# Fourier stage on sums and differences of mirrored tokens, its tables split once into DRAM, and one quarter of the last layer's gate and up weights left unsplit

## The chip, the cores and the metric

One core of one Trainium2 chip runs the program. The metric is the device time of one execution in microseconds (us); less is better. The engines are named as in the profile: PE (TensorE, matmuls), PEld (its weight loads), DVE (VectorE), ACT (ScalarE), POOL (GpSimd), SP (the engine whose queue starts most transfers).

## What is computed

The reference is two blocks on 1024 tokens of 1024 features with 256 context tokens. The first block (attention, RWKV and an MLP) is hardly touched here. The second has two layers; each projects the normalised tokens, mixes them in three ways (a gated chunk MLP, a Fourier mix, attention with four heads), projects back and adds 16 experts that each choose 128 tokens. What the change touches is the Fourier mix and the experts:

```python
def fourier_mix(pf):
    b, n, _ = pf.shape
    f = pf.reshape(b, n, FNET_GROUPS, FNET_GROUP_DIM).astype(jnp.float32)
    y = jnp.fft.fft2(f, axes=(1, 3), norm="ortho").real
    return y.reshape(b, n, FNET_W).astype(pf.dtype)

def chunk_mlp(pu, pv, sgu_norm, w_sgu, b_sgu):
    b, n, _ = pu.shape
    u = jax.nn.gelu(pu)
    v = rms_norm(jax.nn.gelu(pv)) * sgu_norm
    v = v.reshape(b, n // CHUNK, CHUNK, SGU_HEADS, SGU_HEAD_DIM)
    z = jnp.einsum('hpq,bcqhd->bcphd', w_sgu, v) + b_sgu.T[:, :, None]
    return u * z.reshape(b, n, SGU_W)

def expert_choice_moe(h, w_router, w_gate, w_up, w_down):
    ...
    xs = jax.vmap(lambda hb, ib: hb[ib])(h, idx)
    hid = jax.nn.silu(jnp.einsum('becd,edf->becf', xs, w_gate)) * jnp.einsum('becd,edf->becf', xs, w_up)
    y = jnp.einsum('becf,efd->becd', hid, w_down) * g[..., None].astype(h.dtype)
```

The Fourier mix takes 256 features in four groups of 64: a transform over the 1024 tokens (and one over the 256 context tokens in layer 0, since the last layer does not need the context), then one over the 64 features of a group, of which the real part stays.

## The kernel before, in words

All values are float32. Most products run in three parts: an operand is split into a rounded half (type fp32r, a cast on ACT) and the rest (a subtraction on DVE), by `split` (L75), and `mm3` (L85, its matmuls are the lines L87, L88, L89) adds high x high, high x low and low x high in PSUM.

A layer of the second block runs as `mixers` (L254: `project_in`, L606, for ten token tiles of 128; then `spatial`, L657; then the attention heads, whose preparation `prep`, L394, turns and normalises queries and keys), `project` (L764: output projection and router), and `experts` (L1002). The order of a stage's instructions on each engine is set by a scheduler that moves ready work ahead of work that waits, except in `experts`, where it is written by hand.

`spatial` holds the Fourier mix and the gate of the chunk MLP. For each of 8 token tiles it loads a 128x512 piece of the cosine table and one of the sine table (`table`, L691: into `draw`, two buffers, split to `dh`, `dl`, three each), and multiplies both with the two feature halves of the tile: 4 outputs `px`, each summed over the 8 tiles in a PSUM bank of its own, 96 matmuls of 512 columns a layer. Only 512 of the frequencies are computed; the others follow by symmetry, and frequency 512 comes from two-column matmuls with an alternating sign vector (`zps`, L706, L707). Then the four `px` are split and multiplied with small 64x64 tables on a block diagonal (`p2`), and written to DRAM as rows of `cat`. The gate (4 heads), the turning of its product `u` and the `p2` products all share one PSUM bank, `zps`. In layer 0 a small copy of the transform follows for the context. All of it stands between the last transposes of `project_in` (`nat`, L650) and the first attention scores (`SA`). Head 0's preparation is called behind `spatial` (two lines below L464) and its PSUM tiles `tps` are another pool of three banks, so the scheduler mixes its matmuls with those of the stage.

`experts` streams the weights through a ring of buffers `raw`, 512 KB for a piece of 2x128 rows and 512 columns; an expert has 12 pieces: 8 of gate and up, alternating in pairs of k, with 4 of down. `fetch` (L1013) issues loads on SP in that order as buffers come free, `cut` (L1023) splits a piece 5 ahead of its use, on ACT and DVE, each fourth on POOL instead of DVE:

```python
h, lo = (xp.tile([P, 2, 512], F32R, name=n, bufs=NS) for n in ("wh", "wl"))
nc.scalar.copy(h, raw)
(nc.gpsimd if ahead or i % 4 == 3 else nc.vector).tensor_tensor(lo, raw, asf(h), op=OP.subtract)
```

`moe_bufs` (L146) holds for each layer the buffers of the ring beside four early ones (18 and 19), of the halves (6) and the pieces that are cut ahead (5). `up` (L1070) multiplies the chosen tokens, gathered by an indirect transfer on POOL (`gather`, L1039) and turned (`turn`, L1045), with gate and up into `pg` and `pu`.

In the first block the part of the input projection that feeds RWKV (L1412) runs over seven groups of columns, whose weights are loaded and split one group ahead.

Of the kernel before, what the change touches and what calls it, by code (L numbers as in the profile page):

```python
# [17 lines left out]
P = 128  # L18
# [124 lines left out]
class Block2(Base):  # L143
    NE = 16
    moe_early = (0, 4)
    moe_bufs = ((18, 6, 5), (19, 6, 5))  # L146
    def consts2(self, pool, dram):
        self.dram = dram
        self.catd = dram.tile([1024, 1280], F32, name="catd")[:]
        for n, s in (("selr", [P, 16]), ("cosC", [P, 8, 64]), ("sinS", [P, 8, 32])):  # L150
            if not hasattr(self, n):
                setattr(self, n, self.load(pool, n, s))

# [100 lines left out]
    def mixers(self, l, last, lp, xin, cin, crows):  # L254
# [209 lines left out]
        self.spatial(l, last, TQ, f, u2, gv, ssv, sgun, bsg)  # L464
# [141 lines left out]
    def project_in(self, t, only_kv, h, fin, wp, pp, W, cqh, cql, ckh, ckl, kr, sskr, f, u2, gv, ssv, qln, kvln):  # L606
# [50 lines left out]
    def spatial(self, l, last, TQ, f, u2, gv, ssv, sgun, bsg):  # L657

        nc, ins = self.nc, self.ins
        with self.pool(f"g{l}", side="right") as cp, self.pool(f"gps{l}", space=PSUM) as pp:  # L660
# [4 lines left out]
            rv = self.rsqrt(cp, ssv[:, :TQ], TQ, 1.0 / 256, 4e-6)  # L665
            gh, gl = (cp.tile([P, TQ, 256], F32R, name=n) for n in ("gh", "gl"))
            for t in range(TQ):
                nc.vector.scalar_tensor_tensor(gv[:, t], gv[:, t], rv[:, t:t + 1], sgun, op0=OP.mult, op1=OP.mult)
                self.split(gh[:, t], gl[:, t], gv[:, t])
            ws = cp.tile([P, 512], F32, name="draw", bufs=2).rearrange("p (a b) -> p a b", a=4)  # L670
            nc.sync.dma_start(ws, ins["w_sguT"][l])
            wsh, wsl = (cp.tile([P, 4, P], F32R, name=n) for n in ("wsh", "wsl"))
            self.split(wsh, wsl, ws)
            dft, dfh = {}, {}
            for n in ("dftCd", "dftSd") + (() if last else ("dftCdc", "dftSdc")):
                dft[n] = self.load(cp, n, [P, P])
                dfh[n] = [cp.tile([P, P], F32R, name=n + m) for m in "hl"]
                self.split_v(*dfh[n], dft[n])
# [3 lines left out]
            alt = self.load(cp, "alt", [P, 2])  # L682
            altr = cp.tile([P, 2], F32R, name="altr")
            nc.vector.tensor_copy(altr, alt)

            def fpair(t):
                h, lo = (cp.tile([P, 2, 256], F32R, name=n, bufs=2) for n in ("fh", "fl"))
                self.split(h, lo, f[:, t:t + 2])
                return h, lo

            def table(src, shape):  # L691
                raw = cp.tile([P, 512], F32, name="draw", bufs=2)
                raw = raw if len(shape) == 2 else raw.rearrange("p (a b) -> p a b", a=2)
                nc.sync.dma_start(raw, src)
                th, tl = (cp.tile(shape, F32R, name=m, bufs=3) for m in ("dh", "dl"))
                self.split(th, tl, raw)
                return th, tl
            for t in range(8):
                if t % 2 == 0:
                    fh, fl = fpair(t)  # L700
                tb = [table(ins[n][t * P:t * P + P, :], [P, 512]) for n in ("dftC", "dftS")]
                for k in range(2):
                    s = slice(k * P, k * P + P)
                    for j in range(2):
                        self.mm3(pX[2 * k + j], fh[:, t % 2, s], fl[:, t % 2, s], tb[j][0], tb[j][1], t == 0, t == 7)
                    nc.tensor.matmul(pN[:, k, :], fh[:, t % 2, s], altr, start=t == 0 and k == 0, stop=False, skip_group_check=True)  # L706
# [30 lines left out]
            for k in range(2):  # L737
                for g0 in range(0, TQ, 4):
                    n = min(4, TQ - g0)
                    ps = pp.tile([P, 4, P], F32, name="zps")  # L740
                    for i in range(n):
                        nc.tensor.transpose(ps[:, i, :], u2[:, g0 + i, k * P:k * P + P], self.ident)
# [1495 lines left out]
```

## Time and profile before

| | us |
|---|---|
| three runs | 4342.38, 4343.26, 4361.83 |
| median of the runs | 4343.26 |
| the profiled execution's own time | 4345.66 |
| its span, first to last instruction | 4343.8 |
| PE busy in it | 3939.3 |
| DVE busy | 2828.5 |
| ACT busy | 1834.9 |
| POOL busy | 1072.7 |

Busy times are of one execution; the engines work beside each other, so they don't add up to the span. A share over the whole span is an average over stages with different limits, so the change is read from the windows of its own stages. In a row of the trace "us" is from an instruction's start to its end; PE's matmuls overlap, so the distance from one start to the next is what one of them costs. "<-" behind an idle time names what ended it. The granted clock of PE is a share of its full speed.

### The profile page before, as it was taken

To read this page: it belongs to the slowest core of one execution; us is meant where nothing else is said; L and a number is where in the kernel's file an instruction comes from. 1 tells how busy PE (TensorE), PEld (TensorE's weight loads), DVE (VectorE), ACT (ScalarE), POOL (GpSimd) and SP (SyncE) were. 2 spreads that over 40 slices of the span, in tenths; PEclk is the share of its full clock that TensorE was granted. 3 is DMA by queue.
4 is the path that set the end of the run, shared out by engine and by line. 5 is a ranking of instruction groups with operands and counts; after the bars stand their busy time and mean duration, and the time that the engine had idled before them with its cause. 6 is when DMAs were issued, how large, how long until landed. Compare 5 with 4: busy or idle time off the path is not lost. (4 is left out here: it accounts for less than half of the span.)

```text
span 4343.8 us, 69748 instructions
## 1 busy us (share of the span) xinstructions
PE 3939.3 (91%) x27068; PEld 3164.2 (73%) x27068; DVE 2828.5 (65%) x5419; ACT 1834.9 (42%) x3590; POOL 1072.7 (25%) x868
## 2 busy tenths in 40 slices
PE   7998989899889999999988899969997979995988
PEld 5874467777657888888967788747775868874776
DVE  5365657677676644445475566677877556666988
ACT  4234334444433311111144566325664346633665
POOL 1000012223222101101031222434544112234554
PEclk9999989999999999999999999989998989997999
DMA  6226755556462323222030202448996020146996
GB/s 244 66 89 192 234 140 129 152 125 132 86 216 108 123 82 98 93 83 68 20 126 24 73 11 66 163 175 291 304 312 201 15 71 12 69 133 227 333 345 204
DMA packets 433204, 611.91 MB, mean 141 GB/s; under 512 B 93888, under 2 KB 259920, under 8 KB 431976
## 3 DMA queue, kind: packets, MB, share of 16 engines
q1 hardware_dynamic: 403800, 527.74, 37.6%
q0 software_dynamic: 29072, 79.70, 6.7%
q8 instruction: 213, 3.49, 0.3%
q14 instruction: 119, 0.97, 0.1%
HBM read 510.29 MB, written 97.05 MB: 140 GB/s over the span
## 5 line engine op out<-in xcount | busy, mean ns | idle before, releaser
L1028 DVE TENSOR_TENSOR wl<-raw,wh 128x1024 fp32r<-128x1024 f32 x284 | 432.3, 1575 | 23.7 <-ACT wh L1027 23.4
L1027 ACT CAST wh<-raw 128x1024 fp32r<-128x1024 f32 x384 | 386.8, 1052 | 86.9 <-PE pg L89 53.0
L1028 POOL TENSOR_TENSOR wl<-raw,wh 128x1024 fp32r<-128x1024 f32 x100 | 265.6, 2661 | 289.4 <-ACT wh L1027 267.6
L87 PE MATMUL pu<-z,uh 128*128 128x256 f32 x1024 | 293.8, 287 | 4.6 <-ACT uh L77 4.6
L89 PE MATMUL pu<-z,ul 128*128 128x256 f32 x1024 | 291.2, 284 | 2.1 <-DVE ul L78 2.1
L88 PE MATMUL pu<-hl,uh 128*128 128x256 f32 x1024 | 291.2, 284 | 0.0
L2070 DVE TENSOR_TENSOR x<-x,pd 128x512 f32<-128x512 f32 x256 | 174.1, 685 | 128.2 <-PE pd L89 128.2
L2042 POOL TENSOR_TENSOR raw<-raw,g 128x1024 f32<-128x1024 f32 x32 | 82.3, 2589 | 639.6 <-DMA raw<-w_mlp_down 639.6
L87 PE MATMUL gps<-wh,hh 128*128 128x512 f32 (+2 forms) x656 | 224.0, 342 | 15.0 <-ACT hh L77 12.3
L89 PE MATMUL gps<-wh,hl 128*128 128x512 f32 (+2 forms) x656 | 220.7, 337 | 0.5 <-POOL hl L1363 0.5
L87 PEld LDWEIGHTS pu<-z,uh 128*128 128x128 f32 x1024 | 197.8, 193 | 14.8 <-issue 5.4
L87 PE MATMUL pd<-dh,ah 128*128 128x512 f32 x512 | 199.8, 390 | 2.2 <-DVE x L2070 2.0
L89 PEld LDWEIGHTS pu<-z,ul 128*128 128x128 f32 x1024 | 197.8, 193 | 2.5 <-DVE ul L78 2.4
L88 PE MATMUL pd<-dl,ah 128*128 128x512 f32 x512 | 199.4, 389 | 0.0
L89 PE MATMUL pd<-dh,al 128*128 128x512 f32 x512 | 199.2, 389 | 0.0
L88 PEld LDWEIGHTS pu<-hl,uh 128*128 128x128 f32 x1024 | 197.9, 193 | 0.1
L77 ACT CAST wh<-raw 128x512 fp32r<-128x512 f32 (+1 forms) x120 | 73.5, 614 | 200.8 <-PE gp L88 77.5
L87 PEld LDWEIGHTS gps<-wh,hh 128*128 128x128 f32 x656 | 129.8, 198 | 29.7 <-ACT hh L77 13.6
L77 ACT CAST dh<-raw 128x1024 fp32r<-128x1024 f32 x32 | 32.2, 1048 | 282.2 <-PE pd L89 276.2
L2059 DVE TENSOR_TENSOR r<-r 128x512 f32<-128x512 f32 x64 | 55.6, 868 | 142.8 <-ACT ah L2058 142.8
L89 PEld LDWEIGHTS gps<-wh,hl 128*128 128x128 f32 x656 | 129.2, 197 | 14.0 <-POOL hl L1363 0.8
L78 DVE TENSOR_TENSOR ptl<-tps,pth 128x512 fp32r<-128x512 f32 (+1 forms) x200 | 110.2, 588 | 34.9 <-ACT pth L77 33.5
(680 smaller groups left out, 12005.5 us busy)
## 6 DMA issues: line engine op xcount, KB each, us to landing
araw<-w_ada SPq DMA_DIRECT2D x144, 512.0 KB
raw<-w_gate SPq DMA_DIRECT2D x128, 512.0 KB
raw<-w_up SPq DMA_DIRECT2D x128, 512.0 KB
raw<-w_down SPq DMA_DIRECT2D x128, 512.0 KB
raw<-w_in SPq DMA_DIRECT2D x100, 256.0 KB
raw<-w_mlp_up SPq DMA_DIRECT2D x32, 512.0 KB
raw<-w_mlp_down SPq DMA_DIRECT2D x32, 512.0 KB
x<-x SPq DMA_DIRECT2D x24, 512.0 KB
```

Source lines behind the costliest of these rows:

```text
L77: nc.scalar.copy(hi, src)
L78: nc.vector.tensor_tensor(lo, src, asf(hi), op=OP.subtract)
L87: mm(ps, lh, rh, start=start, stop=False)
L88: mm(ps, lh, rl, start=False, stop=False)
L89: mm(ps, ll, rh, start=False, stop=stop)
L1027: nc.scalar.copy(h, raw)
L1028: (nc.gpsimd if ahead or i % 4 == 3 else nc.vector).tensor_tensor(lo, raw, asf(h), op=OP.subtract)
L2042: nc.gpsimd.tensor_tensor(raw2, raw2, g2, op=OP.mult)
L2059: nc.vector.tensor_tensor(r, r, r, op=OP.mult)
L2070: nc.vector.tensor_tensor(x[:, t, s], x[:, t, s], p, op=OP.add)
```

## The change

It has four pieces.

1. *Mirrored tokens.* Cosine is even and sine odd in the token number, so token n and token 1024-n can be added for the cosine table and subtracted for the sine table, ahead of the products. `project_in` writes the second half of the Fourier features to DRAM (`fd`, four transfers on SP); `mirrored` gathers a tile of them in reverse order by an indirect transfer on POOL with an index table `back`; DVE forms sum (`fe`) and difference (`fo` in `r`), which are split. Four token tiles are left instead of eight, so 48 matmuls `px` a layer. Token 512 is its own mirror and is added by four matmuls of one row (`mid`). The two-column matmuls fall from 32 to 16; the last small product, `p3`, is made in three parts.
2. *Tables split once.* `tables` splits six tables of 128x2x512 beside the RWKV projection of the first block, one behind the weights of each of its first six column groups, and stores the halves in DRAM; `spatial` loads them ready (`dt`, 512 KB each, three buffers, 8 a layer and 3 small ones).
3. *More banks.* The gate's outputs and the turned `u` use `tps`, the three banks that head 0's preparation uses too; `p2` reuses the banks of `px`; gate and turning are written between the `p2` products. The reciprocal root `rv`, the products `gv` and their splits are written inside the first of the four iterations and behind it.
4. *Layer 1's experts.* The first pair of k of gate and of up (pieces 0 and 1 of an expert's 12) is not cut: PE reads `raw` and an unsplit copy `xf` of the tokens, two plain float32 matmuls for each piece in place of six. The ring has 18 buffers instead of 19 beside the early ones.

The diff, cut to its core:

```diff
-    moe_bufs = ((18, 6, 5), (19, 6, 5))
+    moe_bufs = ((18, 6, 5), (18, 6, 5))
...
+    def tables(self, ap):
...
+        for a in range(6):
+            raw = ap.tile([P, 2, 512], F32, name="traw")
+            nc.sync.dma_start(raw, ins["dftT"][a] if a < 5 else ins["dftD"])
+            h, lo = (ap.tile([P, 2, 512], F32R, name="tp", bufs=2) for _ in range(2))
+            self.split(h, lo, raw)
+            if a < 5:
+                for m, t in enumerate((h, lo)):
+                    nc.sync.dma_start(self.tabs[a][:, :, m], asf(t))
...
+            yield
...
             nc.vector.tensor_copy(f[:, t], pq[:, :256])
+            if 4 <= t < 8:
+                nc.sync.dma_start(self.fd[(t - 4) * P:(t - 3) * P], f[:, t])
...
+            def mirrored(a):
+                x = cp.tile([P, 256], F32, name="r", bufs=2)
+                nc.gpsimd.indirect_dma_start(out=x, out_offset=None, in_=self.fd,
+                                             in_offset=bass.IndirectOffsetOnAxis(ap=self.back[:, a:a + 1], axis=0))
+                return x
+
+            def table(src, shape=[P, 2, 512]):
+                t = cp.tile(shape, F32R, name="dt", bufs=3)
+                nc.sync.dma_start(asf(t), src)
+                return t
+            r = {3: mirrored(3), 2: mirrored(2)}
+            tb = [table(self.tabs[3][:, j]) for j in range(2)]
...
-            for t in range(8):
-                if t % 2 == 0:
-                    fh, fl = fpair(t)
-                tb = [table(ins[n][t * P:t * P + P, :], [P, 512]) for n in ("dftC", "dftS")]
+            for a in (3, 2, 1, 0):
+                first, end = a == 3, a == 0
+                x, y = cp.tile([P, 256], F32, name="fe"), r.pop(a)
+                nc.vector.tensor_tensor(x, f[:, a], y, op=OP.add)
+                nc.vector.tensor_tensor(y, f[:, a], y, op=OP.subtract)
+                eo = []
+                for n, v in (("fe", x), ("fo", y)):
+                    eo.append((small(n + "h"), small(n + "l")))
+                    self.split(*eo[-1], v)
+                if a >= 2:
+                    r[a - 2] = mirrored(a - 2)
+                if not first:
+                    tb = [table(self.tabs[a][:, j]) for j in range(2)]
                 for k in range(2):
                     s = slice(k * P, k * P + P)
                     for j in range(2):
-                        self.mm3(pX[2 * k + j], fh[:, t % 2, s], fl[:, t % 2, s], tb[j][0], tb[j][1], t == 0, t == 7)
+                        h, lo = eo[j]
+                        self.mm3(pX[2 * k + j], h[:, s], lo[:, s], tb[j][:, 0], tb[j][:, 1], first, end)
...
+                if first:
+                    for k in range(2):
+                        s = slice(k * P, k * P + P)
+                        for m in mid:
+                            nc.tensor.matmul(pX[2 * k], m[:, s], alt[0:1], start=False, stop=False)
+                    rv = self.rsqrt(cp, ssv[:, :TQ], TQ, 1.0 / 256, 4e-6)
...
-                    ps = pp.tile([P, 8, 64], F32, name="zps")
+                    ps = tps.tile([P, 8, 64], F32, name="tps", bufs=3)
...
-                    p2 = pp.tile([P, 512], F32, name="zps")
-                    self.mm3(p2, *dfh[nm], xh, xl, True, True)
+                    gate(2 * k + 1 - j)
+                    p2 = pp.tile([P, 512], F32, name=f"px{2 * k + j}")
+                    self.mm3(p2, dfh[:, 0, j], dfh[:, 1, j], xh, xl, True, True)
...
+            def whole(i):
+                return last and piece_of[i] < 2
+
             def cut(n, ahead=False):
                 while count[1] < min(n, len(plan)):
                     raw, i = raws.pop(0), count[1]
+                    if whole(i):
+                        parts.append((None, None, raw))
+                        count[1] += 1
+                        continue
...
+                    if whole is not None and k0 == 0:
+                        nc.scalar.copy(whole, ps[:, 0:2])
...
                         for j in range(2):
-                            self.mm3(dst, xh[:, k0 + j], xl[:, k0 + j], w[0][:, j], w[1][:, j], k0 + j == 0, k0 + j == 7)
+                            if w[0] is None:
+                                nc.tensor.matmul(dst, U["xf"][:, k0 + j], w[2][:, j], start=k0 + j == 0, stop=False)
+                            else:
+                                self.mm3(dst, xh[:, k0 + j], xl[:, k0 + j], w[0][:, j], w[1][:, j], k0 + j == 0, k0 + j == 7)
...
                 for c0, cn, tiles in groups:
                     W = weights(wp, c0, cn, 8)
+                    next(beside, None)
```

How instructions stand on the engines, before and changed, at three places. The first is PE at the start of layer 0's Fourier stage; `wkh`, `ckh` are operands of head 0's keys, `dt` a split table. Before:

```order
L650 MATMUL nat<-ident,nat 128x128 x3
L87 MATMUL tps<-wkh,ckh 128x256 x2
L88 MATMUL tps<-wkl,ckh 128x256
L89 MATMUL tps<-wkh,ckl 128x256
L87 MATMUL tps<-wkh,ckh 128x256
L88 MATMUL tps<-wkl,ckh 128x256
```

With the change:

```order
L675 MATMUL nat<-ident,nat 128x128 x3
L87 MATMUL px_22875<-dt,feh 128x512
L88 MATMUL px_22875<-dt,feh 128x512
L89 MATMUL px_22875<-dt,fel 128x512
L87 MATMUL px_22876<-dt,foh 128x512
L88 MATMUL px_22876<-dt,foh 128x512
L89 MATMUL px_22876<-dt,fol 128x512
```

Head 0's key and query matmuls, 30 of 256 columns and 60 of 192, now stand behind the whole stage, with only the last small products of the context between them.

The second place is POOL at the same point, where before the turning of the keys' rope part (`krr`) ran without a break. With the change:

```order
L390 TENSOR_TENSOR krr<-kr,kn_roper 128x640
L401 MEMSET k_22828 64x1280
L591 TENSOR_TENSOR krt<-krr,sinS 128x16x16
L592 TENSOR_TENSOR krt<-krr,sinS 128x16x16
L694 DMA r<-fd,back 128x256
L593 TENSOR_TENSOR krr<-krr,cosC 128x512
L694 DMA r<-fd,back 128x256
L594 TENSOR_TENSOR krr<-krr,krt 128x16x16
```

The gathers of mirrored tokens (L694) stand behind four of these operations and between the others. On DVE the whole reciprocal root and six of the products `gv` stand ahead of the first sum `fe`.

The third place is PE at the start of an expert of layer 1. Before:

```order
L1056 MATMUL tps<-ident,xg 128x128 x8
L87 MATMUL pg<-wh,xh 128x512
L88 MATMUL pg<-wl,xh 128x512
L89 MATMUL pg<-wh,xl 128x512
L87 MATMUL pg<-wh,xh 128x512
L88 MATMUL pg<-wl,xh 128x512
```

With the change:

```order
L1116 MATMUL tps<-ident,xg 128x128 x8
L1145 MATMUL pg<-raw,xf 128x512 x2
L1145 MATMUL pu<-raw,xf 128x512 x2
L87 MATMUL pg<-wh,xh 128x512
L88 MATMUL pg<-wl,xh 128x512
```

Four unsplit matmuls stand where twelve of the three-part kind stood, directly behind the transposes of the gathered tokens.

## Rows read from the trace of the kernel before

**Rows 1.** the page's first part: busy us, share of the span, instructions
```profile
PE 3939.3 (91%) x27068; PEld 3164.2 (73%) x27068; DVE 2828.5 (65%) x5419; ACT 1834.9 (42%) x3590; POOL 1072.7 (25%) x868
```

**Rows 2.** windows of layer 0's Fourier stage: engines' busy us, granted clock, DMA
```profile
2367.00:2384.40 17.40, 4.63 (x21) 3.89 (x19) 15.73 (x36) 9.52 (x28) 7.76 (x7) 0.71 0.19 53
2384.40:2428.00 43.60, 37.31 (x165) 28.93 (x165) 26.93 (x61) 17.94 (x49) 3.99 (x2) 0.88 0.38 111
2428.00:2463.60 35.60, 27.13 (x163) 21.78 (x164) 17.99 (x40) 19.02 (x53) 7.58 (x9) 0.96 0.22 80
```

**Rows 3.** windows of layer 1's Fourier stage, same columns
```profile
3489.00:3504.60 15.60, 4.53 (x20) 3.99 (x19) 14.02 (x31) 7.75 (x22) 7.75 (x7) 0.59 0.12 37
3504.60:3548.00 43.40, 38.54 (x170) 29.93 (x170) 23.14 (x54) 18.25 (x54) 4.42 (x2) 0.91 0.35 99
3548.00:3575.60 27.60, 19.02 (x97) 14.90 (x95) 15.14 (x31) 14.80 (x37) 6.92 (x8) 0.78 0.23 84
```

**Rows 4.** window of layer 1's experts, then the DMA view of it
```profile
4040.00:4280.00 240.00, 213.86 (x947) 171.02 (x946) 216.51 (x181) 161.43 (x182) 137.30 (x57) 0.96 1.01 346
...
GB/s 400 419 329 362 344 359 224 396 409 288 258 409 413 298 405 406 282 325 402 328 265 393 412 216 263 406 414 340 362 368 372 249 400 332 280 315 413 349 240 386
...
raw<-w_down SPq DMA_DIRECT2D x47, 512.0 KB
```

**Rows 5.** timeline of PE: start, us, line, operation, tile
```profile
221.42 0.39 PE L88 MATMUL nps<-hl,wh 128*128 128x512 f32 x1
221.65 0.40 PE L89 MATMUL nps<-hh,wl 128*128 128x512 f32 x1
221.89 2.51 PE L1453 MATMUL gps<-sq,bd 128*128 128x512 f32 x6
224.04 0.47 PE L87 MATMUL nps<-hh,wh 128*128 128x256 f32 x1
```

**Rows 6.** timeline of PE, layer 0: the first product with a table
```profile
2384.42 0.73 PE L87 MATMUL px<-dh,fh 128*128 128x512 f32 x2 [1.69 <-ACT dh L77]
```

**Rows 7.** timelines of POOL and of DVE at that start
```profile
2375.34 1.67 POOL L570 TENSOR_TENSOR krr<-krr,cosC 128x512 f32<-128x512 f32 x1
...
2379.20 1.67 DVE L668 SCALAR_TENSOR_TENSOR gv<-gv,ny,sgu_norm_2r 128x256 f32<-128x256 f32 x4
```

**Rows 8.** timelines of POOL and PE: gathers of rows in layer 1's experts
```profile
3989.74 0.97 POOL L1042 DMA_INDIRECT xg<-hn,idx  x1 [0.30 <-issue]
...
3992.83 1.97 PE L1056 MATMUL tps<-ident,xg 128*128 128x128 f32 x8 [5.71 <-DMA xg<-hn,idx]
...
4054.32 6.10 POOL L1042 DMA_INDIRECT xg<-hn,idx  x1 [0.31 <-issue]
```

**Rows 9.** groups of ACT in layer 0's stage from 2397: busy us, mean ns
```profile
L431 ACT ACTIVATE junk<-tps 128x192 f32<-128x192 f32 x10 | 3.4, 343 | 0.1
...
L429 ACT COPY qn<-tps 128x384 f32<-128x384 f32 x5 | 2.4, 485 | 4.9 <-PE tps L89 4.9
...
L431 ACT ACTIVATION_READ_ACCUMULATOR junk<-tps 128x1 f32 x10 | 2.1, 208 | 0.0
...
L415 ACT ACTIVATE junk<-kn 128x128 f32<-128x128 f32 x4 | 1.3, 321 | 0.0
```

**Rows 10.** window of the first block's second projection, columns as rows 2
```profile
170.00:330.00 160.00, 160.00 (x793) 128.28 (x792) 91.43 (x63) 50.74 (x69) 1.71 (x30) 1.00 0.25 87
```

**Rows 11.** waits in layer 1's experts: us in total, times, longest
```profile
PE pu L88 <- POOL wl L1028: 13.3, 4, 4.4
...
PE pg L88 <- DVE wl L1028: 8.4, 6, 1.9
PE pu L88 <- DVE wl L1028: 7.5, 6, 2.0
```

**Rows 12.** timeline of SP's queue in layer 1's experts
```profile
4056.19 0.37 SPq L1019 DMA_DIRECT2D raw<-w_up  x1
4062.82 0.37 SPq L1019 DMA_DIRECT2D raw<-w_gate  x1
```

More of the change, by code (lines that the diff above doesn't have):

```diff
@@ L149, in consts2 @@
         self.catd = dram.tile([1024, 1280], F32, name="catd")[:]
+        self.fd = dram.tile([512, 256], F32, name="fd")[:]
+        self.back = self.load(pool, "back", [P, 4], dt=I32)
+        self.par = self.load(pool, "par", [P, 2])
         for n, s in (("selr", [P, 16]), ("cosC", [P, 8, 64]), ("sinS", [P, 8, 32])):
@@ new lines, in table @@
+            def table(src, shape=[P, 2, 512]):
[4 more added lines that the diff above has]
+            tb = [table(self.tabs[3][:, j]) for j in range(2)]
+            part = lambda n: cp.tile([P, 512], F32R, name=n, bufs=2)
+            alt = part("dl")
+            nc.sync.dma_start(asf(alt), self.taba)
+            par = cp.tile([P, 2], F32R, name="par")
@@ L733, in spatial @@
                 p3 = pp.tile([P, 2], F32, name="zps")
-                nc.tensor.matmul(p3, dft["dftCd"], xn[:, k, :], start=True, stop=True)
+                self.mm3(p3, dfh[:, 0, 0], dfh[:, 1, 0], xn[0][:, k], xn[1][:, k], True, True)
                 nc.vector.tensor_copy(y[:, 0:1], p3[:, 0:1])
                 put()
[L737 to L742, printed above, removed]
-                    y, put = piece(k, g0 * P, n * P)
-                    nc.scalar.mul(y[:, :n * P], ps.rearrange("p a b -> p (a b)")[:, :n * P], 0.5)
-                    put()
+                turned(k)
@@ L746, in spatial @@
             if not last:
-                fh, fl = fpair(8)
-                tb = [table(ins[n].rearrange("(t p) n -> p t n", p=P), [P, 2, 256]) for n in ("dftCc", "dftSc")]
+                fh, fl = (part(n).rearrange("p (t c) -> p t c", t=2) for n in ("dh", "dl"))
+                self.split(fh, fl, f[:, 8:10])
+                tb = [table(self.tabs[4][:, j]).rearrange("p m (t n) -> p m t n", t=2) for j in range(2)]
+                dfc = table(self.tabd[:, :, 2:4], [P, 2, 2, P])
                 for k in range(2):
@@ L1011, in experts @@
             raws, parts, count = self.raws, [], [len(self.raws), 0, 0]
+            piece_of = [i for e in range(NE + 1) for i in (list(range(8)) if e < NE else []) + (list(range(8, 12)) if e else [])]
             def fetch(n):
@@ L1043, in gather, with turn @@
                 return xr
-            def turn(xr, parts=True, to=None):
+            def turn(xr, parts=True, to=None, whole=None):
                 if to is not None:
@@ L1177, in experts @@
             xc = None if last else turn(xc, False, xt[1])
-            U = dict(e=0, x=turn(rows.pop(0), True, xt[0]), xc=xc)
+            unsplit = lambda: xp.tile([P, 2, P], F32, name="xf", bufs=2) if last else None
+            xf = unsplit()
+            U = dict(e=0, x=turn(rows.pop(0), True, xt[0], xf), xc=xc, xf=xf)
             prev = None
@@ L1187, in experts @@
                 if e + 1 < NE:
-                    nxt["x"] = turn(rows.pop(e + 1))
+                    nxt["xf"] = unsplit()
+                    nxt["x"] = turn(rows.pop(e + 1), whole=nxt["xf"])
                     if not last and e % 4 == 3:
@@ L1411, in inproj2 @@
                          [(2304, 160, [(12, 0, 64), (13, 64, 96)])]
+                beside = self.tables(wp)
                 for c0, cn, tiles in groups:
                     W = weights(wp, c0, cn, 8)
+                    next(beside, None)
                     for mi, o, M in tiles:
```

111 lines of the change are left out of this document (60 added, 51 removed).

## The prediction

> **What bounds the kernel now.** I read the page's first part, then the windows of the three places that the change touches, then the waits in the experts, then single rows. The first part says that TensorE (PE) is busy for 91% of the span and DVE for 65% [rows 1], so a saved instruction counts only where PE runs it or waits for it.
>
> The windows cut the Fourier stage of layer 0 (last transposes of the projection to the first scores) in three [rows 2]. Their columns say that PE is busy for 4.63 + 37.31 + 27.13 = 69.1 of 96.6 us; the reader should see that only the first 17.4 us are nearly empty, and that the granted clock is under 1 throughout. Busy time by granted clock gives the work at full clock: 4.63 x 0.71 + 37.31 x 0.88 + 27.13 x 0.96 = 62.2 us. So the stage is 62.2 us of work, 6.9 us that the clock takes, and 27.5 us of idle (12.8 at the start, 6.3 in the middle, 8.5 at the end). Layer 1 by the same sum [rows 3]: 86.6 us are 52.6 of work, 9.5 of clock and 24.5 of idle (11.1, 4.9, 8.6).
>
> The experts of layer 1 are another kind of stage: in 240 us of them PE is busy for 213.9, DVE for 216.5, and the DMA share is 1.01 at 346 GB/s [rows 4]. Three resources are nearly full at once, so what is taken from one meets the next soon.
>
> **The Fourier stage.** Per layer 48 of 96 `px` matmuls of 512 columns go. Neighbouring rows at full clock start 0.23 us apart [rows 5], so, at 0.228, that is 48 x 0.228 = 10.9 us of PE. Sixteen two-column matmuls fewer are set against the four added for the middle token and the p3 products in three parts. Layer 0 keeps 51.3 us of work, layer 1 41.7.
>
> *Start.* Before, the first `px` runs at 2384.42 [rows 6]. Now it needs a gathered mirror tile, a sum and a cast. The first gather stands on POOL ahead of the cosine product, so it is issued where that started, 2375.34 [rows 7]; issue and landing take 3.1 us where the trace shows such a gather with PE waiting for it, from 3989.74 to 3992.83 [rows 8], so it is there by 2378.5. DVE is later: its list has the whole reciprocal root and six `gv` products ahead of the first sum, and these start at 2379.20, 1.67 us for four [rows 7], so 0.42 each. Six products, a sum and a cast at that price put the first `px` at 2382.5: 15.5 us of empty PE from 2367. In layer 1, where the first window is 1.8 us shorter, 14.
>
> *Clock.* The losses of the middle and last windows stay: 5.6 us in layer 0, 7.7 in layer 1.
>
> *End.* This is the part that the change makes worse. Head 0's preparation now stands on PE behind the whole stage, where before it filled gaps between `px` matmuls. Its chain on ACT is 10 key squares of 0.321 us, 3.2, then 3.4 + 2.1 + 2.4 for the queries [rows 9], 11.1 in all; with the readouts, copies and transposes that have no row here I take 18, an estimate. PE has 30 matmuls of 256 columns and 60 of 192 to run meanwhile, 3.4 + 5.1 = 8.5 us, so about 10 us are idle in layer 0 and 9 in layer 1 (two query tiles fewer). In the middle I take half of before's idle, 3 and 2 us: no table has to be cut there any more, and gate and turned outputs have three banks, but the `p2` chain is as serial as before.
>
> *Sum.* Layer 0: 15.5 + 51.3 + 5.6 + 13 = 85.4, against 96.6: **-11 us**. Layer 1: 14 + 41.7 + 7.7 + 11 = 74.4, against 86.6: **-12 us**. The idle is the unknown: none of it after the start would give -24 and -23; a preparation that takes 25 us, with the middle idle as before, gives about 0. Taken is the value nearest to the rows of the preparation [rows 9].
>
> **The tables.** Six loads of 512 KB, six pairs of splits and 13 stores stand beside a projection of the first block in which PE is 100% busy at clock 1.00, while DVE is busy for 91 and ACT for 51 of 160 us [rows 10]. DVE's mean instruction there is 91.43 / 63 = 1.45 us, so its six cuts are about 9 us, and the transfers are 6 MB beside 87 GB/s. PE never waits there, so idle time of the other two hides nearly all: **+1 us**. Bounds: 0, and 9 if every cut on DVE came in front of a matmul that waits. SP issues the table loads between weight loads; those are two tiles ahead, so I price that at nothing.
>
> **The experts of layer 1.** Per expert one quarter of gate's and of up's weights stays unsplit: 2 casts and 2 subtractions go, and 4 unsplit matmuls stand for 12. The only rows of unsplit 512-column matmuls are three with 1282 columns together from 221.89 to 224.04 [rows 5]: 2.15 us, 0.859 per 512 columns, against 3 x 0.228 = 0.684. That costs 0.175 x 64 = 11.2 us of PE. The Trainium skill ("FP8 and Floating Point Precision", section TensorE Precision Notes) counts four passes for a true FP32 product; four times 0.228 would be 0.912 and the sum 14.6 us, 3.4 more; the row lies under it, and the row is taken.
>
> On the other side PE waited for DVE's `wl` for 8.4 us in `pg` and 7.5 in `pu`, and for POOL's for 13.3 [rows 11]. The unsplit pieces are the first two of each twelve, both cut by DVE before, and they stand where an expert begins. I take all of DVE's 15.9 as gone, and half of POOL's, 6.6, because POOL's cuts wait for casts and ACT has 2 of 12 fewer. That is 22.5 - 11.2: **-11 us**. Ends: both kinds of wait gone and some clock with them, -20; none gone, +11.
>
> **The sum**: -11 - 12 + 1 - 11 = -33. The profiled execution took 4345.66 us, 2.4 more than the median of the runs, 4343.26; 4345.66 - 33 - 2.4 = **4310 us**. About 0.5%, 22 us, is what a measurement of this kernel can tell from no change.
>
> **The rivals.**
> *Loads hold the experts.* DMA is full in that stage: share 1.01 [rows 4]. If the transfers set the pace, PE's shorter waits are only moved to the loads, and the longer matmuls may come on top: +11 in place of -11, 4332 us. For it: the share, and the ring has one buffer less. Against it: slices of the same stage moved up to 419 GB/s [rows 4], so 346 isn't a ceiling, and SP's queue issues nothing for 6.6 us from 4056.19 to 4062.82 [rows 12], which a queue that is behind would not. The Trainium skill ("DMA: Bandwidth & Descriptors", section Specifications) states a limit of some 358 GB/s per core on the side of the memory; by it the stage would be 3% from its floor and this rival the forecast. The slices at 400 and over speak against that rule here. Chance 0.12.
>
> *The Fourier stage gives nothing.* The preparation's 18 us become 25 and the start is late, because one gather takes 6.10 us on POOL in place of 0.97, as one row shows [rows 8], and POOL's own list waits behind it. Then the halved work turns into idle: 4310 + 23 = 4333. For it: ACT and POOL have long serial pieces there; against it: that slow gather stood in the stage with full DMA, and this one has a share of 0.19 to 0.38 [rows 2]. The change would then not do what it says for the time. Chance 0.11.
>
> *The Fourier stage gives twice as much.* Banks and tables remove the idle behind the start, and the preparation overlaps the last products: 24 us more, 4286. For it: DVE and ACT lose 18 table cuts each in layer 0 and are no longer busy beside the preparation. Chance 0.15.
>
> *Slower: whole pieces hold their buffers.* An unsplit piece frees its buffer when PE has used it, five pieces later than a cut one. The queue issues 47 loads of w_down in the 240 us [rows 4], 4 for each expert, so an expert lasts 20.4 us and one of its 12 pieces 1.7, and the buffer comes 8.5 us later. SP issues in order; if a load waits for that buffer, all loads behind it wait too. It decides only if transfers in flight run out before; then about half of the 8.5 us is lost in each of 15 experts, 60 us, and the gain of the experts with it: 4310 + 11 + 60 = 4381. For it: gaps of 6.6 us exist [rows 12]; against it: during them the DMA share stays at 1.01 [rows 4], so they are covered now. Chance 0.07.
>
> **How the numbers follow.** Forecast 0.55, its own range 4296 to 4327 (stage parts off by half, experts by 5): 0.45 of it under 4321.5, 0.10 above. Faster: 0.45 + 0.15 + 0.05 of the first rival (4321 if the loads give back only the experts' gain) = 0.65. Same: 0.10 + 0.07 + 0.11 = 0.28. Slower: 0.07. The range goes to both Fourier rivals and the loads: 4282 to 4335; it leaves out the slower case and the joint ends of the bounds.
>
> **What would show it.** Right: 48 `px` matmuls a layer; first `px` some 15.5 us after the last transposes; some 18 to 20 us from the last `p2` to the first scores with PE half busy; the stages near 85 and 74 us; no wait of `pg` or `pu` for DVE at an expert's start; unsplit matmuls at 0.86 us; the projection with the tables as long as before. Wrong: SP gaps over 10 us with a DMA share under 0.9, `px` waiting for gathers or tables, a projection longer by over 3 us, or an end of the stage over 25 us.

## The result and the profile after

The changed kernel takes 4283.63 us (median of 4 runs, 4277.35 to 4290.56), the kernel before 4349.02 in the runs beside it (4 runs, 4342.38 to 4361.83): a ratio of 0.9844, 95% interval 0.9822 to 0.9865. It is faster by 1.6%, where 0.8% was forecast. The profiled execution took 4277.35 us, its span is 4275.5, 68.3 under that of before.

The first part of the page answers to [rows 1]; DVE has 91 us less to do, PE only 28:

```profile
PE 3910.9 (91%) x26888; PEld 3129.5 (73%) x26888; DVE 2737.0 (64%) x5375; ACT 1792.2 (42%) x3558; POOL 1062.6 (25%) x874
```

Cut at the starts of four kinds of PE rows (last transposes `nat` of the projection, first scores `SA`, first transposes of an expert's tokens, the end), the two profiles give:

| stretch, us | before | after | difference | forecast |
|---|---|---|---|---|
| first block, layer 0's projection | 2366.8 | 2371.0 | +4.2 | +1 |
| layer 0's Fourier stage | 96.9 | 72.0 | -24.9 | -11 |
| layer 0's attention to the experts | 453.5 | 459.4 | +5.9 | 0 |
| layer 0's experts, layer 1's projection | 571.5 | 574.3 | +2.8 | 0 |
| layer 1's Fourier stage | 86.9 | 67.3 | -19.5 | -12 |
| layer 1's attention to the experts | 417.3 | 419.9 | +2.6 | 0 |
| layer 1's experts | 351.0 | 311.6 | -39.4 | -11 |

The windows that answer to [rows 2 to 4], layer 0's stage, layer 1's, then the experts (PE, PEld, DVE, ACT, POOL busy; granted clock, DMA share, GB/s):

```profile
2371.20:2386.00 14.80, 0.26 (x3) 0.01 (x1) 13.43 (x26) 5.27 (x15) 9.25 (x9) 0.59 0.41 142
2386.00:2405.00 19.00, 16.88 (x71) 13.18 (x71) 13.56 (x38) 6.11 (x16) 2.11 (x2) 0.87 0.56 179
2405.00:2442.90 37.90, 31.13 (x213) 26.16 (x213) 21.97 (x58) 25.32 (x84) 10.71 (x11) 0.99 0.29 103
3476.90:3493.00 16.10, 0.50 (x4) 0.27 (x3) 14.72 (x30) 6.61 (x18) 9.21 (x9) 0.59 0.46 163
3493.00:3510.00 17.00, 16.96 (x73) 13.13 (x73) 11.21 (x30) 3.97 (x11) 5.25 (x4) 0.89 0.57 189
3510.00:3544.00 34.00, 25.32 (x147) 20.15 (x147) 17.61 (x48) 21.87 (x72) 8.85 (x8) 0.86 0.18 68
4020.00:4260.00 240.00, 239.33 (x1039) 182.10 (x1038) 184.29 (x182) 158.55 (x193) 139.91 (x63) 1.00 1.01 360
```

Two things are to be seen. In the experts PE has no idle time left (239.3 of 240, clock 1.00, against 213.9 and 0.96 in [rows 4]) while DVE fell from 216.5 to 184.3. In both Fourier stages PE is nearly empty in the first window (0.26 of 14.8 us, 0.50 of 16.1) and nearly full in the middle one (16.88 of 19.0, 16.96 of 17.0).

Where the experts of before lost their time shows in the distance between two experts' first transposes. In the order of the experts: 13.9, 13.4, 19.2, **25.8**, 19.4, 19.2, 20.4, **25.8**, 19.6, 19.2, **25.8**, 18.1, 21.5, 20.0, 23.9. After: 14.4, 13.9, and then 18.4 thirteen times. The timeline of before in the first 25.8, DVE, POOL and PE beside the gather of [rows 8] at 4054.32 that lasted 6.10 us (start, length):

```profile
4052.68 6.88 DVE L1028 TENSOR_TENSOR wl<-raw,wh 128x1024 fp32r<-128x1024 f32 x6
...
4060.45 4.66 POOL L1028 TENSOR_TENSOR wl<-raw,wh 128x1024 fp32r<-128x1024 f32 x2
...
4062.85 0.80 PE L88 MATMUL pu<-wl,xh 128*128 128x512 f32 x1 [4.41 <-POOL wl L1028]
```

DVE runs six cuts without a gap until 4059.56; the gather ends at 4060.42, and POOL's own cut, for which PE waits 4.41 us, comes behind it. (A cut is here the subtraction that makes the low half of a piece.) In the changed kernel all of these gathers last 0.9 to 1.2 us. The groups of DVE's cuts from 4020 to 4260 (busy us, mean ns), before:

```profile
L1028 DVE TENSOR_TENSOR wl<-raw,wh 128x1024 fp32r<-128x1024 f32 x101 | 167.9, 1719 | 2.3 <-ACT wh L1027 2.2
```

and after:

```profile
L1087 DVE TENSOR_TENSOR wl<-raw,wh 128x1024 fp32r<-128x1024 f32 x93 | 126.2, 1403 | 18.0 <-ACT wh L1086 17.8 <-DMA raw<-w_down 0.3
```

The same cut, whose shortest rows are 1.21 us in both, costs DVE 1.72 us in the mean before and 1.40 after, and now DVE has idle time before it. The single rows say where the rest goes: of the 101 cuts before, the 58 that overlap no cut of POOL's last 1.21 us, none over 1.23, and the 43 that overlap one last 2.40 in the mean. After, the 51 that overlap one last 1.56.

### The profile page after: what moved, and what is told of

Its sections match the earlier page's. It is cut to its first block, busy times and chain, and to the rows that moved or that the text cites. A ratio compares the mean times of both kernels' runs of the same rounds, so it can differ in the third digit from the quotient of the medians.

```text
span 4275.5 us, 69296 instructions
## 1 busy us (share of the span) xinstructions
PE 3910.9 (91%) x26888; PEld 3129.5 (73%) x26888; DVE 2737.0 (64%) x5375; ACT 1792.2 (42%) x3558; POOL 1062.6 (25%) x874
## 5 line engine op out<-in xcount | busy, mean ns | idle before, releaser
L1086 ACT CAST wh<-raw 128x1024 fp32r<-128x1024 f32 x352 | 354.7, 1053 | 77.8 <-PE pg L89 51.7
L1087 DVE TENSOR_TENSOR wl<-raw,wh 128x1024 fp32r<-128x1024 f32 x254 | 347.7, 1417 | 42.1 <-ACT wh L1086 41.5
L2114 POOL TENSOR_TENSOR raw<-raw,g 128x1024 f32<-128x1024 f32 x32 | 83.8, 2635 | 636.8 <-DMA raw<-w_mlp_down 544.4
L87 PE MATMUL gps<-wh,hh 128*128 128x512 f32 (+2 forms) x656 | 224.2, 342 | 18.5 <-ACT hh L77 14.2
L87 PEld LDWEIGHTS pu<-z,uh 128*128 128x128 f32 x1024 | 197.1, 192 | 14.8 <-issue 5.4
L77 ACT CAST wh<-raw 128x512 fp32r<-128x512 f32 (+1 forms) x120 | 73.5, 614 | 204.2 <-PE gp L88 80.3
```

The costliest lines, as they stand in the source:

```text
L77: nc.scalar.copy(hi, src)
L87: mm(ps, lh, rh, start=start, stop=False)
L2114: nc.gpsimd.tensor_tensor(raw2, raw2, g2, op=OP.mult)
```

## The experiments

All ratios are to the kernel before on the same chip. "Stages" are the two Fourier stages, "experts" is layer 1's stretch, in the profile of that run.

**One part alone.** *fourier_only* undoes the unsplit pieces and has the ring's 19 buffers again; *unsplit_only* puts them alone into the kernel before, with 18 buffers. The line of *fourier_only*:

```diff
-                return last and piece_of[i] < 2
+                return False
```

> The changed kernel with the experts of layer 1 as they were before (all pieces cut, 19 buffers); the Fourier stage and the tables stay changed. By the traces, the stretch of layer 1's experts got 39 us shorter and the two Fourier stages 44 us, and some 15 us were lost elsewhere. If these add up, the gain of this kernel over before is about 30 us (4349 to about 4320) and its experts take 351 us as before. Rival: the experts gained because the Fourier change left something better for them (other transfers, an earlier start); then they stay well under 351 us here, and the kernel stays under 4300.

> The kernel before with only the unsplit pieces in layer 1's experts (and 18 buffers). If the parts add up: experts 312 us, the whole about 4310; the first block as before, since the tables are not split there. Rival (the experts' gain depends on the Fourier change): experts over 330 us.

*fourier_only*: 4314.33 us, ratio 0.9886 (0.9857 to 0.9914), stages 73.3 and 67.8, experts 350.4, with the 25.8 us distances as before. *unsplit_only*: 4317.27 us, 0.9888 (0.9857 to 0.9919), stages 98.8 and 87.0, experts 311.2. By the stretches the parts add up, and neither needs the other. Over the whole kernel they give 46 and 43 us, 89 together, where the change gave 65 and, run again, 81 (*changed_again*); what makes that difference stays open. The first block took 2378.9 us in *unsplit_only*, without the tables in it.

**Which pieces.** *late_pair*:

```diff
-                return last and piece_of[i] < 2
+                return last and piece_of[i] in (4, 5)
```

> The changed kernel, but with the third pair of k of gate and up unsplit (pieces 4 and 5 of an expert's 12) instead of the first. Both kinds take two cuts of nine from DVE. Theory pace: before, DVE's cuts set the pace of layer 1's experts (216.5 of 240 us busy), so which two go does not matter: experts 312 us, within 5. Theory start: the gain is that an expert's first products no longer wait for a cut and cover the splits of its tokens, which only the first pair can do; then less than half of the gain is left here, experts over 330 us.

4282.5 us, 0.9821 (0.9786 to 0.9856), experts 315.6, all inner distances 18.4 or 18.5. Where in the expert the unsplit pair stands hardly matters: the theory of the start falls.

**The cuts given back.** *dve_load_back* and *cut_back* leave PE as in the change:

```diff
                     if whole(i):
+                        wd = xp.tile([P, 2, 512], BF16, name="wd")
+                        nc.scalar.copy(wd, raw)
+                        nc.vector.tensor_tensor(wd, raw, wd, op=OP.subtract)
```

(dve_load_back has no copy and subtracts raw from itself.)

> The changed kernel, with a subtraction of 128x1024 on DVE for each unsplit piece put back, whose result nobody reads (raw minus itself into a bf16 tile), so PE's products and their operands are those of the change and only DVE's time is given back, 2.4 us an expert. Theory pace: the experts fall back to the pace of DVE, 345 us or more (with the longer products up to 11 more than before). Theory start: they stay near 312 us, since no product at an expert's start waits for it. Between: 325 to 340 us if DVE's pace matters only where POOL's cuts meet it.

> The changed kernel with both halves of the cut put back for the unsplit pieces, a cast on ACT and a subtraction on DVE of 128x1024 each, whose results nobody reads. With DVE's subtraction alone the experts of layer 1 took 336 us, 25 of the 39 gained. Theory pace of the whole cutting chain (cast, then subtraction, in the order of the pieces): now the chain is that of before and the experts take 351 us or more, up to 362 with the longer products. Theory DVE alone: they stay at 336, and what is left of the gain comes from the products at an expert's start that wait for no cut.

*dve_load_back*: 4304.9 us, 0.9867 (0.9834 to 0.99), experts 336.4; two of its gathers last 6.10 us again, and the distances there are 23.6 and 24.3. *cut_back*: 4311.95 us, 0.99 (0.9867 to 0.9932), experts 342.2, under the 351 to 362 expected. DVE's 2.4 us an expert return 25 of the 39 us, ACT's cast 6 more. The rest was not taken apart.

**Without gathers on POOL.** *plain_rows* is the kernel before, reading the first 128 tokens for every expert:

```diff
+                if last:
+                    nc.sync.dma_start(xr, src[0:P])
+                else:
+                    nc.gpsimd.indirect_dma_start(out=xr, out_offset=None, in_=src, in_offset=bass.IndirectOffsetOnAxis(ap=ix, axis=0))
```

> The kernel before, but layer 1's experts read the same first 128 tokens by a plain transfer on SP in place of the gather of their chosen tokens on POOL, so the experts work on the wrong tokens; the bytes are the same, and the scatter at the end stays on POOL. Before, 4 of the 15 distances between two experts' starts are 25.8 us against 19 to 20, and in those POOL's gather lasts 6.1 us in place of 1 to 1.6, while DVE runs six subtractions without a gap; POOL's cut behind it is late and PE waits for it. Theory lockout (the gather can't finish while DVE runs without a gap): the 25.8 us distances are gone, all are 18.5 to 20.5, and the experts take 351 - 4 x 6.4 = 325 us. Rival (the gather is only late with the rest, and DVE's cuts themselves are the delay): distances of 25 us stay, experts over 340 us.

4354.09 us, 0.9992 (0.9969 to 1.0014), experts 355.4. A miss for the lockout theory as it was put: the slow gathers are gone, and the experts are no shorter; their inner distances are 17.7 to 23.2, all but one of them 20.0 or more. (The expectation counts four distances of 25.8 before; there are three, and one of 23.9.) Its window shows why:

```profile
4020.00:4260.00 240.00, 213.69 (x959) 170.41 (x958) 235.51 (x182) 161.74 (x185) 108.50 (x46) 0.97 0.98 339
```

DVE is busy for 235.5 of 240 us with the same number of instructions, 182. The slow gathers delayed some experts, but DVE was behind anyway: while POOL is held up by a gather DVE cuts in 1.2 us, and otherwise the two slow each other. Here 66 of DVE's 101 cuts overlap one of POOL's, where 43 did before, and these last 2.31 us in the mean.

**All cuts on DVE.** *dve_cuts_before* is the kernel before, *dve_cuts_after* the changed one, with:

```diff
-                    (nc.gpsimd if ahead or i % 4 == 3 else nc.vector).tensor_tensor(lo, raw, asf(h), op=OP.subtract)
+                    (nc.gpsimd if ahead or (i % 4 == 3 and not last) else nc.vector).tensor_tensor(lo, raw, asf(h), op=OP.subtract)
```

> The kernel before with all cuts of layer 1's experts on DVE, none on POOL behind the start: 12 instead of 9 an expert. Theory exclusion (a DVE cut lasts 1.21 us alone, 1.7 in the mean before because POOL's cuts of 2.5 us keep it out): 12 x 1.21 + 5 us of other work = 19.5 us an expert of DVE, distances of 19 to 20 us, no slow gathers' 25 us beyond what gaps allow, experts 330 to 345 us, at or under before's 351. Theory count (each cut costs DVE 1.7 us whatever POOL does): 12 x 1.7 + 5 = 25 us an expert, experts over 400 us.

> The changed kernel with all cuts of layer 1's experts on DVE: 10 an expert. Theory exclusion: 10 x 1.21 + 5 = 17.1 us of DVE, under PE's 18.4, so the distances stay 18.4 us and the experts 312. Theory count: 10 x 1.4 (its mean in the change) + 5 = 19 us, distances of 19 us or more, experts over 320.

*dve_cuts_before*: 4308.53 us, 0.9895 (0.9871 to 0.9918), experts **307.5**: with no piece unsplit, and three more cuts an expert on DVE, they are shorter than in the change. Its window and its cuts on DVE:

```profile
4020.00:4260.00 240.00, 238.29 (x1125) 196.04 (x1124) 237.26 (x253) 187.04 (x216) 119.70 (x25) 1.00 1.03 373
```

```profile
L1028 DVE TENSOR_TENSOR wl<-raw,wh 128x1024 fp32r<-128x1024 f32 x157 | 180.4, 1218 | 0.3 <-ACT wh L1027 0.3
```

157 cuts at 1.218 us take 180.4 us of DVE, where 101 beside POOL's took 167.9. Every gather from the fifth on lasts 8.3 to 8.4 us there. In the rows below it ends 0.86 us behind DVE's run of eight cuts, as the one of before did behind its six. That costs the experts nothing that shows, since no cut stands behind it on POOL:

```profile
4044.07 8.31 POOL L1042 DMA_INDIRECT xg<-hn,idx  x1 [0.30 <-issue]
...
4042.36 9.16 DVE L1028 TENSOR_TENSOR wl<-raw,wh 128x1024 fp32r<-128x1024 f32 x8
```

*dve_cuts_after*: 4272.59 us, 0.9812 (0.9775 to 0.9849), experts 312.7, distances 18.4: PE is the bound there, and POOL's share is not needed.

**Half the unsplit pieces.** *half_dose*, `piece_of[i] < 1`, and *early_half*, the same with the early gathers of below:

> The changed kernel with only gate's first pair unsplit (piece 0), up's first pair cut again. PE's work falls by 0.35 us an expert, DVE gets one cut of 1.2 us back. If one piece is enough to give DVE gaps: distances of 18.1 us, experts 306 us, 5 less than the change. If DVE runs without gaps again: slow gathers come back in some experts, distances of 24 us among them, experts 320 to 335 us, as with DVE's two subtractions given back (336).

> The early gathers together with the one unsplit piece. The early gathers gave 1.2 and 2.6 us in the two stages; with 5 us from the experts the whole is some 9 us under the changed kernel (about 4274 where that has 4283). If half a dose brings slow gathers back, it is 10 to 20 us over it.

*half_dose*: 4278.42 us, 0.9808 (0.9768 to 0.9848). The distances fall to 18.0, yet the experts take 311.0: the last one starts earlier, and 47.6 us pass from there to the end in place of 43.6. *early_half*: 4272.31 us, 0.9798 (0.9758 to 0.9837), experts 312.1. The chain that ended last in the changed kernel says what stands at the end:

```profile
4228.81 1.15 DVE wl L1087
4229.95 10.74 DMA raw<-w_up
4240.76 12.51 DMA raw<-w_down
```

The last loads do: with PE at its pace the transfers end the stage, and their share was 1.01 in the window above. In *dve_cuts_before*, with 19 buffers, the chain ends in DVE's cuts instead.

**The Fourier stage.** *one_bank* puts gate, turning and `p2` back into `zps`; *split_in_stage* drops `tables` and splits the half tables in the stage; *mirrored_only* does both:

```diff
-                    ps = tps.tile([P, 8, 64], F32, name="tps", bufs=3)
+                    ps = pp.tile([P, 8, 64], F32, name="zps")
...
-                t = cp.tile(shape, F32R, name="dt", bufs=3)
-                nc.sync.dma_start(asf(t), src)
+                t = cp.tile(shape, F32R, name="dt", bufs=2)
+                raw = cp.tile([P, 512], F32, name="draw", bufs=2)
...
+                nc.sync.dma_start(raw, src)
+                self.split(t[:, 0], t[:, 1], raw)
```

> The changed kernel with the gate's outputs, the turned products and the p2 products in one PSUM bank (zps) again. That bank also holds the alternating sums until the last token tile, so the gate can't run between the table products. Theory banks: the stages grow by 5 to 9 us each (72 to about 79 in layer 0, 67 to about 73 in layer 1). Rival: the gain of the stages is all from the halved products and ready tables; then they stay within 2 us.

> The changed kernel without the tables in DRAM: the half tables are loaded raw and split in the stage, on ACT and DVE, with two buffers of 512 KB instead of three (there is no room for more), and nothing stands beside the first block's projection. Theory feed: 8 to 10 cuts of 0.62 and 0.69 us a layer come back in front of the products, and the stages grow by 4 to 8 us each. Rival: with half the tables the cuts fit beside PE, the stages grow by less than 2 us, and the tables in DRAM were not needed. In both cases the first block should not get shorter by more than what its length differs between runs (12 us so far).

> The changed kernel with both the one bank and the splitting in the stage back, so that of the Fourier change only the sums and differences are left. Alone the bank cost 6.6 us in layer 0 and 0.5 in layer 1, the splitting 2.8 and 0.9. If these add: stages of 81 and 69 us, so the mirrored tokens give 16 and 18 of the 25 and 20 us. If they stand in for each other (a late table is hidden behind a late gate): 79 and 68 or less. If each hides the other's cost now (both late): over 84 and 71.

| | us | ratio (interval) | stages |
|---|---|---|---|
| one_bank | 4282.11 | 0.9823 (0.9792 to 0.9855) | 78.6, 67.8 |
| split_in_stage | 4280.82 | 0.9819 (0.9787 to 0.9851) | 74.8, 68.2 |
| mirrored_only | 4290.02 | 0.9837 (0.9795 to 0.988) | 80.8, 76.8 |

Against the first profile of the change the bank is worth 6.6 us in layer 0, the tables 2.8, and the mirrored tokens the other 16 of 25. But in the eight profiles that have the Fourier stage of the change as it is, layer 0's took 72.0 to 74.0 us (mean 73.3), so the bank's share is 5 to 7 and the tables' 1 to 3. In layer 1 bank and tables alone are worth under 1 us each, and together 9.5; the same eight profiles took 65.8 to 73.5 there (mean 69.1, see below), so that sum stays open. The tables in DRAM buy little once there are half as many.

*early_gather* issues the first two gathers inside the projection:

```diff
+                    if t in (5, 6):
+                        r[8 - t] = mirrored(8 - t)
```

> The changed kernel with the first two gathers of mirrored tokens issued two tiles earlier, inside the projection, as soon as the rows that they read are written, into a tile that does not share memory with the projection's. In the changed kernel PE is idle for 16 us at each stage's start, since the gather stands behind four operations of POOL and the sum behind the reciprocal root and six gate products. Theory start: the sum then runs ahead of the root, the first product comes some 7 us after the last transposes, and each stage is 7 to 9 us shorter (layer 0 from 72 to 64, layer 1 from 67 to 59). Rival: the gate then becomes late and the saved time turns into waits in the middle; the stages stay within 2 us.

4271.66 us, 0.9809 (0.9776 to 0.9843). The first `px` comes 7.8 us after the last transposes in place of 16.1, as expected, but the stages are 70.8 and 64.7, only 1 to 3 us shorter than in the first profile of the change (2 and 4 by the means of the three profiles with early gathers and the eight without): mostly the rival. Layer 1's windows in it:

```profile
3468.00:3476.00 8.00, 3.55 (x10) 2.98 (x11) 7.57 (x16) 3.42 (x10) 6.44 (x5) 0.58 0.67 252
3476.00:3495.00 19.00, 15.50 (x54) 11.67 (x53) 15.15 (x40) 5.25 (x15) 4.15 (x5) 0.73 0.44 146
3495.00:3533.00 38.00, 29.11 (x169) 23.11 (x168) 19.27 (x51) 23.05 (x74) 10.23 (x10) 0.88 0.22 77
```

PE starts 8 us sooner and then is granted 0.73 of its clock where the change has 0.89 (0.71 and 0.74 in *best* and *early_half*), and idles 3.5 us there, 2.5 of them for the gate's halves. Time saved at the start came back as a slower clock and a later gate.

**What the runs point to.** *best* has the changed Fourier stage, early gathers, no unsplit piece and all cuts on DVE; *changed_again* is the changed kernel beside it:

> What the runs point to: the changed Fourier stage with the early gathers, and layer 1's experts with every piece split as before (19 buffers) but all cuts on DVE. Stages of 71 and 65 us, experts 307.5 us; 6 to 8 us under the changed kernel if these add up. Rival: the experts' gain without unsplit pieces needs the kernel before around it; then they take over 312 us and this is level with the changed kernel.

> The changed kernel once more, beside the one above. Stages of 72 and 67 us, experts 312 us again; the rest of the time differs by up to 20 us between executions, of which the first block's length (2364 to 2387 us so far, with and without the tables) should be the larger part.

*best*: 4264.99 us (5 runs), 0.9794 (0.9779 to 0.9809), stages 70.6 and 65.3, experts 308.7. *changed_again*: 4279.8 us, 0.982 (0.9802 to 0.9838), stages 73.8 and 73.5, experts 311.9. *best* beats the kernel before. Under the change it lies by some 15 us of the medians, but the two intervals overlap, so that it beats the change is likely and not shown; in the experts the gain is 3 us. *changed_again*'s long stage in layer 1 comes from one gather and the sum that waits for it:

```profile
3484.65 4.55 POOL L694 DMA_INDIRECT r<-fd,back  x1 [4.27 <-DVE fol L78]
...
3494.95 0.42 DVE L724 TENSOR_TENSOR fe<-f,r 128x256 f32<-128x256 f32 x1 [5.67 <-DMA r<-fd,back]
```

In the first profile of the change this gather took 2.87 us. The eight profiles fall into these two cases: with 2.87 us (five of them) the stage took 65.8 to 67.8 us, with 4.55 (three) 71.9 to 73.5. In *changed_again* the gather stands beside a run of DVE's sums and subtractions without a gap and ends 0.87 us behind it, as in the experts; in the first profile it ended inside the same run. What decides between the two is open; it is worth some 5 us of this stage.

## Why the prediction was right and wrong

*Direction and range held*, the range by luck: 4283.63 lies just inside 4282 to 4335, and faster had 0.65. The size did not: 33 us were forecast and 65 to 68 measured. The three stretches that the change aims at became 83.8 us shorter, where 34 were forecast. The 15.5 us that the other stretches lost, much of which is what they differ by between executions, brought the time back inside the range.

*The experts' term failed*, -11 against -39.4. Its price for PE was right: an unsplit matmul costs 0.86 us, rows of four records (two matmuls) take 1.72 us. The step that failed is "I take all of DVE's 15.9 as gone, and half of POOL's, 6.6". It took a part of the named waits at PE for the loss, and nothing for the clock. What there was to lose stands in the windows from the third expert's first transposes to the last one's, thirteen distances, before and after:

```profile
4020.10:4298.10 278.00, 247.82 (x1094) 197.69 (x1093) 254.40 (x209) 184.98 (x208) 157.89 (x65) 0.96 0.99 337
```

```profile
3992.30:4231.90 239.60, 239.60 (x1041) 182.03 (x1040) 183.25 (x183) 158.93 (x195) 140.78 (x65) 1.00 1.03 365
```

Before, PE idled 30.2 us and the clock took some 0.04 x 247.8 = 9.9 more. All of that went, because PE, once fed, has neither idle time nor a lowered clock. 1.7 us came back as more work: -38.4, and start and end give the rest. The price of the unsplit matmuls would have been 9.1 for these thirteen experts; why only 1.7 show was not taken apart. The prediction's own window had it: 26.1 us of idle and 8.6 of clock in 240 [rows 4]. (An expert lasted 278.0 / 13 = 21.4 us there, not the 20.4 that the prediction took from counted loads.) The end of -20 in the bounds was too small for the same reason. The prediction had the row of the slow gather [rows 8] and priced it in the Fourier rival; it did not ask what DVE did in those 6 us, nor who stood behind the gather on POOL.

*What paced the experts*: not the number of DVE's cuts, as *dve_cuts_before* shows, but that DVE's and POOL's instructions hold each other up. Taking two cuts from DVE (the change), or three from POOL, frees both.

*The Fourier stage*, -23 forecast and -44.4 measured: near its rival of 47 (24 more). By the forecast's own sum layer 0 was to be 51.3 us of work, 5.6 of clock and 28.5 of idle; the windows after give 0.26 x 0.59 + 16.88 x 0.87 + 31.13 x 0.99 = 45.7, 2.6 and 23.4. In layer 1 work was 4.5 us less than forecast, the clock's share 2 less, the idle about as forecast. So of the 21 us more, 10 are work, 5 clock and 6 idle. The rival laid all of it on the idle, so its number came near by luck. Over the eight profiles the two stages took 73.3 and 69.1 us in the mean, and 97.4 and 86.4 in the four with the stage of before, so the gain is nearer to 41.

The start was right (15.5 of idle forecast, first `px` 16.1 us after the last transposes), and for the reason given: DVE's root and six products stood ahead of the first sum, which started at 2386.20, right behind them. The gather's 3.1 us were misread, from the second gather's start to the first one's landing (the first started at 3988.41, 4.4 us); it did not matter, since DVE was later. Two steps failed. "Layer 0 keeps 51.3 us of work, layer 1 41.7" was too much by 5.6 and 4.5: the sixteen two-column matmuls that were set against small additions had cost some 0.2 us each before, at the low clock, which is a part of it; the rest was not taken apart. "The losses of the middle and last windows stay" failed too: in layer 0 the middle is granted 0.87 as against 0.88 before, but PE is busy there for 16.88 us in place of 37.31, and the last window is granted 0.99 in place of 0.96. The idle at the end was 6.8 us, not 10.

*The tables* cost nothing that shows: the first block took 2364.0 to 2387.2 us in twelve profiles with them (mean 2371.9) and 2366.8 to 2384.3 in six without (mean 2376.1). Much of the other stretches' +11 us in the first table is of that kind: layer 0's attention took 451.7 to 459.4 us over all profiles. Layer 1's took 411.0 to 417.5 in the four profiles with the Fourier stage of before and 415.7 to 423.4 in the other fourteen (means 415.2 and 419.4), so some 4 us there may be a cost of the change; no run takes it apart.

*The rivals*: whole pieces holding their buffers did not cost what was feared: the longest gap between two loads in the stage is 7.2 us, against 6.6 before. The loads did not set the pace of the experts in the change either, though they end the stage. In *half_dose*, with PE faster by 0.4 us an expert, 60 of the chain's 64 us from 4201.1 to 4265.2 are loads, and the stage is hardly shorter (311.0 us).

## What to carry to other kernels

Price a stage's loss from its window (idle plus what the clock takes), not from a part of the waits that a list names: when the thing that paces a stage goes, all of it can go, as in these experts. It need not: in layer 0's Fourier stage 23.4 of 27.5 us of idle stayed. Where two engines share one job, compare the mean of an instruction with its shortest row; 1.72 us against 1.21 says that the second engine's help is paid for by the first, and giving the whole job to one may be faster than either split. An earlier start is worth only what the next wait leaves of it: 8 us at the head of the stage brought 2 to 4.

## What the runs showed of the hardware

DVE's cuts (two inputs in SBUF) and POOL's run longer beside each other: DVE's 1.21 us alone and up to 4.1 beside POOL's, POOL's 2.36 alone and 2.74 in the mean beside DVE's. POOL's gather was held up while DVE ran such subtractions without a gap: 6.10 us beside six cuts, 8.31 beside eight, 0.9 to 1.6 otherwise in the experts of before. It is not a rule without exception: a gather of mirrored tokens ended after 2.87 us inside such a run. The Trainium skill ("SBUF — State Buffer", section SBUF: two separate sides) says that the two engines have one pair of ports in common, held whole by one of them for an instruction, and that POOL can't write a transfer's descriptors while DVE copies in a mode that uses both ports. The rows of the cuts agree in kind with the first. For the second the page says that `tensor_tensor`, which these cuts are, did not stall a transfer; the gathers of 6.10 and 8.31 us beside them say otherwise, and the measurement decides.

Over the 240 us of *dve_cuts_before* the core moved 373 GB/s, above the limit of about 358 that the Trainium skill gives ("DMA: Bandwidth & Descriptors", section Specifications), so that limit did not bind here.
